# Fixed places in a block for rotation, norm steps and turns; POOL's weight splits in halves; fill 4.2: a hybrid attention and S5 block

## The chip, the cores and the metric

One core of a Trainium2 chip. The metric is the device time of one execution in microseconds (us), the median of several runs. Everything is float32; matrix products run in a three-product scheme (below).

## The reference

One layer over x (1024 tokens × 1024 channels). Beside the attention branch it has an S5 branch with its own gate and up projection, which the change doesn't touch.

```python
h = rmsnorm(x) * (1 + scale) + shift                 # adaLN from c
q, k, v, z_a, u, z_s, g_a, g_s = split(h @ w_in)
q, k = partial_rope(q), partial_rope(k)              # 4 heads, 2 parts each, 64 wide
p = softmax(q k^T * 64**-0.5)                        # per part, per head
o = (p[0] - lam * p[1]) @ v                          # v: 128 wide per head
o = rmsnorm(o, g_subln) * (1 - lam_init)
attn_branch = (o * silu(z_a)) @ w_up_attn
merged = sigmoid(g_a) * attn_branch + sigmoid(g_s) * ssm_branch
out = rmsnorm(x + gate * (merged @ w_out), g_final)
```

## The kernel before

The kernel writes its order of work by hand, engine by engine. Its engines are TensorE (PE: matmuls and transposes), VectorE (V in the code, DVE in the profile), ScalarE (A, ACT), GpSimd (G, POOL) and SyncE (SP, whose queue issues most DMAs). Each engine works through its own instructions in program order.

**Products.** Each float32 operand is split into a high part (a copy by ScalarE, rounded) and a low part (the rest, by a subtract), and a product is three matmuls: high × high, high × low, low × high. The helper `split` (L104) does copy and subtract. Weights come through a plan of 1024-column tiles: `w_load` (L166) issues a tile's DMA, `w_split` (L178) splits it on the engine that `w_state["eng"]` names, and `w_ahead` (L200) does both one unit in advance, after the first triple of the running unit. A unit (`unit`, L209) makes 128 rows of a projection in two halves of 512 tokens; each half has 8 triples of matmuls and yields 0.66 after each.

**Main and fill.** `drive` (L233) runs a main generator, whose yields add to a budget, and spends the budget on a fill generator, whose yields take from it. So the fill's matmuls are woven into the main's order on PE at fixed places.

**The attention stage** (`s3_main`, L1523) has 4 heads of 8 blocks; block g = 8h + i holds 128 queries. Its order for block g:

- `qk(g)` (L1410): the scores of both parts (8 matmuls), their maxima by DVE, their exponentials e by ScalarE;
- `mix(g-1)` (L1436) on DVE: a reciprocal, the weight w (wm), and e[0] + w · e[1] over 1024 columns, "the mix" here;
- in odd blocks `pv` (L1460), 24 matmuls for two blocks' outputs of P·V, copied by ScalarE;
- `spot(0)`, fill, `spot(1)`, fill;
- `transpose_w(g-1)` (L1446): 8 transposes of the mix into two PSUM banks (tag `tp`, two buffers), each evacuated by ScalarE (wth) and DVE (wtl);
- fill, `spot(2)`, fill.

The yields of a block are FA ± FD and FB: 3.1 + 1.0 = 4.1 on average up to block 23 (one more in even blocks, one less in odd ones), and 2.45 + 1.0 from block 24 on. Blocks 32 and 33 finish the last mixes and P·V without scores.

**Fill.** In heads 0 to 2 the fill (`s3_fill`, L1401) makes the next head's q, k and v, then five units of the gate g_a, which go to DRAM through tiles tagged `stg`. For q and k each half has a rotation and a cut (`rope_unit`, L1309). The rotation `turn` is a shuffle by DVE and three POOL operations on 128x512 (sh·sin, q·cos, the sum); `cut` is a copy by ScalarE (rh) and a subtract by POOL, and `finish` then issues four DMAs on SP's queue. They are put off: `ev` appends them to the queue `pend` as turn, skip, skip, cut, and `with_pend` (L1303) pops one at every second yield of the fill. `flush` empties the queue at a head's first block. Head 0's q, k and v come ahead of the blocks, on DVE.

**Places in a block.** `spot(s, g)` (L1531) does, in heads 1 to 3: at (block i = 2, s = 0) V's turn `make_v`; at (2, 1) the previous head's output turn `o_turn` (8 transposes into the same two `tp` banks, copied by ScalarE); at each later spot one step of the norm `o_norm` (L1482); at (5, 0) the load of z; at (6, 0) the turn back `o_back` (L1509: 8 transposes, then two DVE operations) and the store to DRAM.

```python
if (i, s) == (2, 1) and h < 4:
    o_turn(h - 1)
    gens[h] = o_norm(h - 1)
elif h in gens and next(gens[h], gens) is gens:
    gens.pop(h)
```

The norm takes squares (ScalarE, two halves through tag `tb`, which the rotation's sh shares), sums (DVE), an inverse square root in twelve steps on 128x8 (three scalings rqv, nri, nry, then three rounds of nrt, nrt, nry) and one product over 128x1024 by POOL.

**The tail** (`s3_tail`, L1586) does the last head's output turn, norm and turn back on DVE, reloads the first three heads, splits them, and spends what fill is left: yields of 3.0 four times, then all. The up projection with w_up_attn follows, then w_out and the final norm.

Of the kernel before, what the change touches and what calls it, by code (L numbers as in the profile page):

```python
# [18 lines left out]
P = 128  # L19
# [47 lines left out]
def tile_hybrid_block(  # L67
# [12 lines left out]
    def mul(o, a, b, e=None):  # L80
        tt(o, a, b, ALU.mult, e)
# [4 lines left out]
    def sub(o, a, b, e=None):  # L86
        tt(o, a, b, ALU.subtract, e)
# [10 lines left out]
    def act(o, i, f, **kw):  # L98
        A.activation(out=o, in_=i, func=f, **kw)  # L99
# [4 lines left out]
    def split(hi, lo, src, lo_eng=None):  # L104
        act(hi, src, AF.Copy)
        sub(lo, src, f32(hi), lo_eng)
# [71 lines left out]
    def w_split():  # L178
        i = w_state["split"]
        if i >= len(plan):  # L180
            return
        r = w_raw.pop(i)
        h = pp.tile([P, 8 * P], F32R, tag="wh", bufs=2, name="wh")
        l = pp.tile([P, 8 * P], F32R, tag="wl", bufs=2, name="wl")
        split(h, l, r, w_state["eng"])
        k = plan[i][2]
        w_hl[i] = tuple(t[:].rearrange("p (k n) -> p k n", k=k) for t in (h, l))
        w_state["split"] += 1
# [1107 lines left out]
    def flush():  # L1296
        while pend:
            pop()

    def skip():  # L1300
        pass

    def with_pend(g, every):  # L1303
        for n, q in enumerate(g):
            if q is not None and n % every == 0:
                pop()
            yield q

    def rope_unit(c0, scale, h, finish):  # L1309
        t = {}  # L1310

        def ev(hf, sl, ps):
            if hf == 0:
                t["q"] = p3.tile([P, S], F32R, tag="ta", bufs=2, name="rq")
            tq = t["q"]
            lo = tq
            q = f32(tq[:, sl])
            e = V if h == 0 else G
            act(q, ps, AF.Copy, scale=scale)

            def turn():
                sh = p3.tile([P, 512], F32, tag="tb", name="rs")
                V.stream_shuffle(out=sh, in_=q, mask=ROPE_SWAP)
                mul(sh, sh, sinT[:, sl], e)
                mul(q, q, cosT[:, sl], e)
                add(q, q, sh, e)

            def cut():
                if hf == 0:
                    t["h"] = p3.tile([P, S], F32R, tag="tc", name="rh")  # L1330
                hi = t["h"]
                act(hi[:, sl], q, AF.Copy)
                sub(lo[:, sl], q, f32(hi[:, sl]), e)
                if h == 0:
                    finish(hi, lo, sl)

            pend.extend([turn, skip, skip, cut])
            if hf == 1 and h > 0:
                pend.append(lambda: finish(t["h"], lo, slice(0, S)))
        yield from unit(c0, 8, hh, hl, ev)  # L1340

    def prep_q(h):
# [67 lines left out]
    def qk(g):  # L1410
        h, i = divmod(g, 8)
        H = heads[h]
        if i == 0:
            flush()
            H["o"] = po.tile([P, S], F32, tag="o", bufs=2, name="o")
            H["zr"] = po.tile([P, 8, 2], F32, tag="zr", bufs=2, name="zr")
        tok = slice(i * P, i * P + P)
        tb = slice(i % 2 * P, i % 2 * P + P)
        nm = po.tile([P, 2], F32, tag="nm", bufs=2, name="nm")
        zz = po.tile([P, 2], F32, tag="zz", bufs=2, name="zz")  # L1420
        es = []
        for cc in range(2):
            sc = ps3.tile([P, S], F32, tag="sc", bufs=2, name="sc")
            for hf in range(2):
                sl = slice(hf * 512, hf * 512 + 512)
                PE.matmul(out=sc[:, sl], lhsT=H["qq"][:, cc, tok], rhs=H["kk"][:, cc, sl], start=True, stop=False)  # L1426
                PE.matmul(out=sc[:, sl], lhsT=qb_t[g // 2][:, cc, tb], rhs=H["kk"][:, cc, sl], start=False, stop=True)  # L1427
            V.tensor_reduce(out=nm[:, cc:cc + 1], in_=sc, axis=AX.X, op=ALU.max, negate=True)  # L1428
            e = p3.tile([P, S], F32, tag="e", bufs=4, name="e")
            act(e, sc, AF.Exp, bias=nm[:, cc:cc + 1], accum_out=zz[:, cc:cc + 1])  # L1430
            es.append(e)
        e_t[g] = (es, zz)
        if g % 2 == 0:
            turn_q(g // 2 + 1)
# [47 lines left out]
    def o_norm(h, e=G, big=None):  # L1482
        H = heads[h]
        on, zr, o = H["on"], H["zr"], H["o"]
        ss = po.tile([P, 8], F32, tag="oss", name="oss")
        z2 = po.tile([P, 8], F32, tag="wm", bufs=2, name="z2")
        for hf in range(2):
            sl = slice(hf * 512, hf * 512 + 512)
            if big is None:
                jk = p3.tile([P, 512], F32, tag="tb", name="sq")  # L1490
            else:
                jk = big[:, sl]
            act(jk, o[:, sl], AF.Square)
            yield
            V.tensor_reduce(out=ss[:, 4 * hf:4 * hf + 4], in_=jk.rearrange("p (t e) -> p t e", t=4) if big is not None
                            else jk[:].rearrange("p (t e) -> p t e", t=4), axis=AX.X, op=ALU.add)
        mul(z2, zr[:, :, 0], zr[:, :, 0])
        mul(ss, ss, z2)
        yield
        res = []  # L1500
        for n, _ in enumerate(rsqrt_gen(po, ss, 8, 1.0 / P, "o", res)):
            if n % 3 == 2:
                yield
        rs = res[0]
        mul(rs, rs, zr[:, :, 0])
        mul(on, on, bc(rs[:], 2, [P, 8, P]), e)
        yield

    def o_back(h):  # L1509
        H = heads.pop(h)  # L1510
        on, of = H["on"], H["of"]
        pss = []
        for hf in range(2):
            ps = ps3.tile([P, 512], F32, tag="tp", bufs=2, name="tp")
            for k in range(4):
                PE.transpose(ps[:, k * P:k * P + P], on[:, hf * 4 + k, :], ident)
            pss.append(ps)
        for hf, ps in enumerate(pss):
            sl = slice(hf * 512, hf * 512 + 512)
            stt(of[:, sl], ps, cols[:, CSUB:CSUB + 1], of[:, sl], ALU.mult, ALU.mult)  # L1520
        return of

    def s3_main():  # L1523
        run_all(with_pend(chain(prep_q(0), prep_k(0), prep_v(0)), 1))
        flush()
        make_v(0)
        w_state["eng"] = G
        NG = 32
        gens = {}

        def spot(s, g):  # L1531
            h, i = divmod(g, 8)
            if g < 8:
                return
            if (i, s) == (2, 0) and h < 4:
                make_v(h)
            if (i, s) == (2, 1) and h < 4:
                o_turn(h - 1)
                gens[h] = o_norm(h - 1)
            elif h in gens and next(gens[h], gens) is gens:  # L1540
                gens.pop(h)
            if (i, s) == (5, 0):
                load_za(h - 1)
            if (i, s) == (6, 0):
                assert h not in gens
                SP.dma_start(out=ofd[h - 1], in_=o_back(h - 1))

        for g in range(NG + 2):
            fa, fb = (FA, FB) if g < 24 else (LA, LB)
            odd = g % 2  # L1550
            fa += FD * (1 - 2 * odd)
            if g < NG:
                qk(g)
            if 1 <= g <= NG:
                mix(g - 1)
            if g >= 3 and odd:
                pv((g - 3) // 2)
            spot(0, g)
            yield fa / 2
            spot(1, g)  # L1560
            yield fa / 2
            if 1 <= g <= NG:
                transpose_w(g - 1)
            yield fb / 2
            spot(2, g)
            yield fb / 2

    FA, FB, FD = 3.1, 1.0, 1.0
    LA, LB = 2.45, 1.0
    fill3 = with_pend(s3_fill(), 2)  # L1570
    drive(s3_main(), fill3)
    p3.release()
    p2.release()
# [12 lines left out]
    def s3_tail():  # L1586
        o_turn(3)
        load_za(3)
        norm = o_norm(3, V, op.tile([P, S], F32, tag="pt", bufs=3, name="sq2"))
        next(norm)  # L1590
        ofl = []
        for h in range(3):
            ofl.append(op.tile([P, S], F32, tag="sg", bufs=3, name="ofl"))
            SP.dma_start(out=ofl[h], in_=ofd[h])
        next(norm)
        yield 3.0
        run_all(norm)
        for h in range(3):
            split(oh[:, h], ol[:, h], ofl[h])
            yield 3.0  # L1600
        of = o_back(3)
        split(oh[:, 3], ol[:, 3], of)
        yield 1000.0
# [124 lines left out]
    def finish(t, rs):  # L1728
        stt(xr[t], xr[t], rs, gf, ALU.mult, ALU.mult)
        SP.dma_start(out=ov[t], in_=xr[t])  # L1730
# [62 lines left out]
```

## Time and profile before

| | us |
|---|---|
| runs | 912.81, 911.06, 912.46 |
| median | 912.46 |
| profiled execution, whole | 911.19 |
| its span, first to last instruction | 909.3 |
| its mean granted clock of PE | 0.989 |
| attention stage, blocks and tail | about 460 to 772 |

The times are those of whole executions. The profile is of one of them, and its microseconds count from the first instruction. Busy times of PE include the overlap of a matmul with the next; a timeline row gives start, length, engine, line, operation, output <- inputs, form and count, and in brackets the idle time of the engine before it and what ended it.

### The profile page before, as it was taken

How to read it: one execution, taken by the hardware profiler on the slowest of the kernel's cores; microseconds unless marked ns; L12 is line 12 of the kernel's file. 1: busy time of each engine (PE TensorE's matmuls, PEld its weight loads, DVE VectorE, ACT ScalarE, POOL GpSimd, SP SyncE). 2: the span in 40 equal slices, each digit the busy share in tenths (PEclk: the TensorE clock that was granted, in tenths of full speed). 3: DMA queues.
4: the chain of work that ended last, by engine and by line, in shares of the span. 5: the costliest groups of instructions: out<-in, count | busy, mean ns of one | idle time of the engine just before them, and what ended most of it. 6: DMA issues, size and time to landing. Idle time of an engine off the chain costs nothing.

```text
span 909.3 us, 12201 instructions
## 1 busy us (share of the span) xinstructions
PE 873.0 (96%) x4528; PEld 732.6 (81%) x4528; DVE 673.3 (74%) x1264; ACT 366.1 (40%) x610; POOL 134.5 (15%) x115
## 2 busy tenths in 40 slices
PE   5999999999999899999999999898999999999996
PEld 4878888888888788787878887787788888887886
DVE  5986999899999976674657767875866756573465
ACT  6754442132222236301246556455555544232222
POOL 1001000000000001000025434423511111350000
PEclk9899899999999999999999999999999999999999
DMA  9936133333243446595433313132232224848022
GB/s 296 307 83 186 52 112 110 101 98 118 85 126 107 125 139 196 207 327 185 123 98 81 91 38 81 64 95 63 70 105 58 81 94 140 333 176 312 12 88 98
DMA packets 107117, 119.56 MB, mean 131 GB/s; under 512 B 7716, under 2 KB 87825, under 8 KB 107059
## 3 DMA queue, kind: packets, MB, share of 16 engines
q1 hardware_dynamic: 105268, 114.08, 40.5%
q10 hardware_dynamic: 1614, 4.51, 1.2%
q8 instruction: 36, 0.59, 0.3%
q0 software_dynamic: 176, 0.20, 0.1%
q14 instruction: 23, 0.18, 0.1%
HBM read 78.46 MB, written 27.73 MB: 117 GB/s over the span
## 4 chain that ended last, share of the span: by engine, by line
PE 41%; DVE 7%; ACT 3%; DMA 2%; issue 2%; POOL 2%; SPq 0%; ACTq 0%; DVEq 0%; POOLq 0%
PE mm L217 19%; PE op L1712 9%; PE pv L1468 4%; PE tp L1457 3%; PE sc L1427 3%; PE sc L1426 2%; DVE nm L1428 2%; POOL pta L78 1%; DVE e L96 1%; ACT e L99 1%; DVE wtl L78 1%; DMA wor<-in_w_out_dram 1%; DMA pad<-pt 1%; ACT mh L99 1%; DMA pta<-pad 1%
## 5 line engine op out<-in xcount | busy, mean ns | idle before, releaser
L217 PE MATMUL mm<-hh,wh 128*128 128x512 f32 x592 | 239.1, 404 | 0.0
L217 PE MATMUL mm<-hh,wl 128*128 128x512 f32 x592 | 232.6, 393 | 2.9 <-DVE wl L78 2.8
L217 PE MATMUL mm<-hl,wh 128*128 128x512 f32 x592 | 232.6, 393 | 0.0
L217 PEld LDWEIGHTS mm<-hh,wl 128*128 128x128 f32 x592 | 112.1, 189 | 28.2 <-DVE wl L78 4.1
L217 PEld LDWEIGHTS mm<-hh,wh 128*128 128x128 f32 x592 | 112.3, 190 | 22.4 <-issue 1.7
L217 PEld LDWEIGHTS mm<-hl,wh 128*128 128x128 f32 x592 | 112.5, 190 | 20.4
L99 ACT ACTIVATE e<-sc,nm 128x1024 f32<-128x1024 f32 x64 | 71.2, 1115 | 77.1 <-DVE nm L1428 77.0
L1428 DVE TENSOR_REDUCE nm<-sc 128x1 f32<-128x1024 f32 x64 | 75.3, 1218 | 14.2 <-PE sc L1427 13.1
L78 DVE TENSOR_TENSOR wtl<-tp,wth 128x512 fp32r<-128x512 f32 x64 | 41.2, 686 | 60.0 <-ACT wth L99 59.9
L99 ACT ACTIVATE wh<-wr 128x1024 fp32r<-128x1024 f32 x49 | 51.7, 1056 | 62.0 <-DMA wr<-in_w_in_dram 24.2
L99 ACT ACTIVATE side<-mm 128x512 f32<-128x512 f32 x48 | 28.7, 598 | 112.8 <-PE mm L217 78.5
L78 POOL TENSOR_TENSOR wl<-wr,wh 128x1024 fp32r<-128x1024 f32 x14 | 34.7, 2477 | 207.2 <-ACT wh L99 207.0
L78 DVE TENSOR_TENSOR wl<-wr,wh 128x1024 fp32r<-128x1024 f32 x35 | 42.9, 1227 | 29.2 <-ACT wh L99 29.0
L1712 PE MATMUL op<-woh,ml 128*128 128x512 f32 (+1 forms) x136 | 51.3, 377 | 1.1 <-DVE ml L78 1.1
L1712 PE MATMUL op<-wol,mh 128*128 128x512 f32 (+1 forms) x136 | 51.2, 377 | 0.0
L1712 PE MATMUL op<-woh,mh 128*128 128x512 f32 (+1 forms) x136 | 51.2, 377 | 0.0
L99 ACT ACTIVATE wth<-tp 128x512 fp32r<-128x512 f32 x64 | 34.8, 596 | 40.1 <-PE tp L1457 40.1
L1426 PE MATMUL sc<-kk,qq 128*128 128x512 f32 x128 | 49.9, 390 | 0.0
L1427 PE MATMUL sc<-kk,qb 128*128 128x512 f32 x128 | 49.9, 390 | 0.0
L96 DVE SCALAR_TENSOR_TENSOR e<-e,wm 128x1024 f32<-128x1024 f32 x32 | 45.3, 1415 | 1.1
L1468 PE MATMUL pv<-wth,vh 128*128 128x256 f32 x128 | 36.5, 285 | 2.7 <-DVE wtl L78 2.7
L1457 PE MATMUL tp<-cst,e 128*128 128x128 f32 x256 | 33.3, 273 | 5.8 <-DVE nry L78 2.4
(365 smaller groups left out, 1693.1 us busy)
## 6 DMA issues: line engine op xcount, KB each, us to landing
wr<-in_w_in_dram SPq DMA_DIRECT2D x40, 512.0 KB
wa<-in_w_ada_dram SPq DMA_DIRECT2D x16, 512.0 KB
x<-in_x_dram SPq DMA_DIRECT2D x8, 512.0 KB
gsd<-side SPq DMA_DIRECT2D x8, 512.0 KB
gad<-side SPq DMA_DIRECT2D x8, 512.0 KB
gt<-gsd SPq DMA_DIRECT2D x8, 512.0 KB
wg<-in_w_ada_dram SPq DMA_DIRECT2D x8, 512.0 KB
pad<-pt ACTq DMA_DIRECT2D x8, 512.0 KB
```

The costliest lines, as they stand in the source:

```text
L78: (e or V).tensor_tensor(out=o, in0=a, in1=b, op=op)
L96: V.scalar_tensor_tensor(out=o, in0=a, scalar=s, in1=b, op0=op0, op1=op1)
L99: A.activation(out=o, in_=i, func=f, **kw)
L217: PE.matmul(out=ps, lhsT=a[:, k, off:off + P], rhs=r[:, k, sl], start=(n == 0), stop=(n == 3 * K - 1))
L1426: PE.matmul(out=sc[:, sl], lhsT=H["qq"][:, cc, tok], rhs=H["kk"][:, cc, sl], start=True, stop=False)
L1427: PE.matmul(out=sc[:, sl], lhsT=qb_t[g // 2][:, cc, tb], rhs=H["kk"][:, cc, sl], start=False, stop=True)
L1428: V.tensor_reduce(out=nm[:, cc:cc + 1], in_=sc, axis=AX.X, op=ALU.max, negate=True)
L1457: PE.transpose(ps[:, k, :], e[:, kt * P:kt * P + P], ident)
L1468: PE.matmul(out=ps[:, 0:256], lhsT=a[:, kt, :], rhs=r[:, kt, :], start=(n == 0), stop=(n == 23))
L1712: PE.matmul(out=ps[:, 0:n], lhsT=a[:, k, tok], rhs=r[:, k, lo:lo + n], start=(i == 0), stop=(i == 23))
```

## The change

- `w_split`: where the split is POOL's, its subtract is made in two operations of 512 columns instead of one of 1024.
- `rope_unit`, heads 1 to 3: each half appends one turn and one cut (with `finish` in the second half's cut). The fill is no longer wrapped in `with_pend`. `pop_turn` at s = 0 of every block runs what is queued up to and including the next turn; `pop_cut` at s = 2 of blocks i = 5 to 7 runs a cut if it is first.
- `spot`: the norm's nine steps stand at nine given places (`STEPS`) of blocks 3 to 7; the output turn goes to (3, 1), the load of z to (7, 0), the turn back with its store to (0, 0) of the next head. `o_norm` has one more yield, and the tail one more `next`.
- FA is 3.2, so a block's yields are 4.2 on average up to block 23.

```diff
@@ w_split
-        split(h, l, r, w_state["eng"])
+        act(h, r, AF.Copy)
+        if w_state["eng"] is G:
+            for j in range(0, 8 * P, 512):
+                sub(l[:, j:j + 512], r[:, j:j + 512], f32(h[:, j:j + 512]), G)
+        else:
+            sub(l, r, f32(h))
@@ behind skip
+    def pop_turn():
+        while pend:
+            kind, fn = pend.popleft()
+            fn()
+            if kind == "turn":
+                break
+
+    def pop_cut():
+        if pend and pend[0][0] == "cut":
+            pend.popleft()[1]()
@@ rope_unit, ev
-            pend.extend([turn, skip, skip, cut])
-            if hf == 1 and h > 0:
-                pend.append(lambda: finish(t["h"], lo, slice(0, S)))
+            def cut_all():
+                cut()
+                if hf == 1:
+                    finish(t["h"], lo, slice(0, S))
+
+            pend.extend([turn, skip, skip, cut] if h == 0 else [("turn", turn), ("cut", cut_all)])
@@ qk
-            flush()
+            while pend:
+                pop_turn()
@@ o_norm
-        z2 = po.tile([P, 8], F32, tag="wm", bufs=2, name="z2")
...
             act(jk, o[:, sl], AF.Square)
             yield
+            if hf == 1:
+                z2 = po.tile([P, 8], F32, tag="wm", bufs=2, name="z2")
             V.tensor_reduce(out=ss[:, 4 * hf:4 * hf + 4], in_=jk.rearrange("p (t e) -> p t e", t=4) if big is not None
                             else jk[:].rearrange("p (t e) -> p t e", t=4), axis=AX.X, op=ALU.add)
+            if hf == 0:
+                yield
@@ s3_main
+        STEPS = ((3, 2), (4, 0), (4, 2), (5, 0), (5, 1), (6, 0), (6, 1), (7, 0), (7, 1))
+
         def spot(s, g):
             h, i = divmod(g, 8)
-            if g < 8:
+            if 1 <= h < 4 and (i, s) in STEPS:
+                next(gens[h], None)
+            if s == 0:
+                pop_turn()
+            if s == 2 and i >= 5:
+                pop_cut()
+            if (i, s) == (0, 0) and h >= 2:
+                SP.dma_start(out=ofd[h - 2], in_=o_back(h - 2))
+            if not 1 <= h < 4:
                 return
-            if (i, s) == (2, 0) and h < 4:
+            if (i, s) == (2, 0):
                 make_v(h)
-            if (i, s) == (2, 1) and h < 4:
+            if (i, s) == (3, 1):
                 o_turn(h - 1)
                 gens[h] = o_norm(h - 1)
-            elif h in gens and next(gens[h], gens) is gens:
-                gens.pop(h)
-            if (i, s) == (5, 0):
+            if (i, s) == (7, 0):
                 load_za(h - 1)
-            if (i, s) == (6, 0):
-                assert h not in gens
-                SP.dma_start(out=ofd[h - 1], in_=o_back(h - 1))
@@ behind s3_main
-    FA, FB, FD = 3.1, 1.0, 1.0
+    FA, FB, FD = 3.2, 1.0, 1.0
     LA, LB = 2.45, 1.0
-    fill3 = with_pend(s3_fill(), 2)
+    fill3 = s3_fill()
@@ s3_tail
         next(norm)
+        next(norm)
         yield 3.0
```

## Rows read from the trace of the kernel before

**Rows 1.** The page, part 1: busy time, share of the span, instructions
```profile
PE 873.0 (96%) x4528; PEld 732.6 (81%) x4528; DVE 673.3 (74%) x1264; ACT 366.1 (40%) x610; POOL 134.5 (15%) x115
```

**Rows 2.** Stretches by windows: length, busy of each engine, clock, DMA share, GB/s
```profile
460.00:752.00 292.00, 280.26 (x1570) 239.71 (x1569) 206.46 (x313) 156.37 (x278) 98.37 (x64) 1.00 0.28 76
```

**Rows 3.** Waits of PE, 455 to 752 us: total us, times, longest us
```profile
PE tp L1479 <- DVE vl L78: 3.2, 3, 1.1
PE pv L1468 <- DVE wtl L78: 2.7, 3, 2.0
PE tp L1457 <- DVE nry L78: 2.4, 2, 1.7
PE tp L1457 <- DVE nrt L78: 2.2, 2, 1.3
```

**Rows 4.** Timeline of PE in block 1: start us, us, engine, line, operation
```profile
467.01 0.39 PE L1426 MATMUL sc<-kk,qq 128*128 128x512 f32 x1
...
470.63 0.39 PE L217 MATMUL mm<-hh,wl 128*128 128x512 f32 x1
472.17 1.09 PE L1457 MATMUL tp<-cst,e 128*128 128x128 f32 x8 [1.15 <-DVE e L96]
```

**Rows 5.** Timeline of POOL in block 12
```profile
566.30 1.29 POOL L78 TENSOR_TENSOR rq<-rq,rs 128x512 f32<-128x512 f32 x1
568.58 2.43 POOL L78 TENSOR_TENSOR wl<-wr,wh 128x1024 fp32r<-128x1024 f32 x1 [0.99 <-ACT wh L99]
```

**Rows 6.** Timeline of DVE in block 12
```profile
566.27 2.40 DVE L96 SCALAR_TENSOR_TENSOR e<-e,wm 128x1024 f32<-128x1024 f32 x1
...
568.78 2.25 DVE L96 SCALAR_TENSOR_TENSOR nrt<-nrt,rqv 128x8 f32<-128x8 f32 x1
```

**Rows 7.** Timeline of DVE in block 1
```profile
468.11 2.35 DVE L1428 TENSOR_REDUCE nm<-sc 128x1 f32<-128x1024 f32 x2 [4.60 <-PE sc L1427]
...
470.83 1.28 DVE L96 SCALAR_TENSOR_TENSOR e<-e,wm 128x1024 f32<-128x1024 f32 x1
```

**Rows 8.** Timeline of DVE at 639 to 645 us, POOL in a rotation from 639.40
```profile
639.23 1.26 DVE L78 TENSOR_TENSOR wtl<-tp,wth 128x512 fp32r<-128x512 f32 x2
...
640.76 1.22 DVE L91 TENSOR_SCALAR nri<-rqv 128x8 int32<-128x8 int32 x1
...
642.09 2.35 DVE L1428 TENSOR_REDUCE nm<-sc 128x1 f32<-128x1024 f32 x2
```

**Rows 9.** The chain that ended last, in order of time: start us, us, what
```profile
589.69 0.87 PE tp L1457 x8
...
593.08 2.87 PE pv L1468 x24
```

**Rows 10.** Groups of POOL by line and form: busy us, mean ns of one, idle before
```profile
L78 POOL TENSOR_TENSOR wl<-wr,wh 128x1024 fp32r<-128x1024 f32 x14 | 34.7, 2477 | 207.2 <-ACT wh L99 207.0
```

**Rows 11.** Timelines at 649 to 652 us, POOL's row first, then DVE's two
```profile
650.80 1.31 POOL L78 TENSOR_TENSOR rs<-rs,sinT 128x512 f32<-128x512 f32 x1
...
649.66 1.22 DVE L96 SCALAR_TENSOR_TENSOR nrt<-nrt,rqv 128x8 f32<-128x8 f32 x1
650.91 1.22 DVE L96 SCALAR_TENSOR_TENSOR nry<-nrt,nry 128x8 f32<-128x8 f32 x1
```

**Rows 12.** Groups of ACT by line, 455 to 752 us
```profile
L99 ACT ACTIVATE e<-sc,nm 128x1024 f32<-128x1024 f32 x64 | 71.2, 1115 | 77.1 <-DVE nm L1428 77.0
...
L99 ACT ACTIVATE rh<-rq 128x512 fp32r<-128x512 f32 x12 | 7.5, 629 | 5.4 <-POOL rq L78 5.4
```

**Rows 13.** Timelines at the stage's end: PE (two rows), then DVE (two rows)
```profile
739.64 1.03 PE L1457 MATMUL tp<-cst,e 128*128 128x128 f32 x8
...
767.63 0.48 PE L217 MATMUL mm<-hh,wh 128*128 128x512 f32 x1
...
740.96 1.29 DVE L78 TENSOR_TENSOR wtl<-tp,wth 128x512 fp32r<-128x512 f32 x2 [2.29 <-ACT wth L99]
...
770.02 1.23 DVE L78 TENSOR_TENSOR ol<-of,oh 128x1024 fp32r<-128x1024 f32 x1 [1.13 <-ACT oh L99]
```

## The prediction

> **What bounds the kernel now.** I began with the page's busy times: TensorE (PE) is busy 96% of the span, DVE 74%, and PEld (81%) only overlaps PE [rows 1]. So a change pays where PE stands still. The stretches by windows show that the attention stage has such time: from 460 to 752 us PE is busy 280.26 of 292.00 us, 11.7 us idle, at a granted clock of 1.00 [rows 2]. The waits of PE give the causes [rows 3]: 3.2 us (3 times) for the subtract that frees the banks of V's turn, 2.7 us (3) for the lower part of the weights of P·V, 2.4 and 2.2 us (2 each) put down to small steps of the norm (nry, nrt); one mix adds 1.15 us [rows 4]. A matmul is drawn 0.39 us long but the next starts 0.23 us later, so each stall takes 0.16 us more than its idle time: the transposes at 472.17 could have begun at 470.86 [rows 4]. These 11 stalls are 11.65 + 11 × 0.16 = 13.4 us, the ceiling of what the change can win here.
>
> Why is VectorE (DVE) late? At 566.30 GpSimd (POOL) makes the third operation of a rotation, 1.29 us, and at 568.58 a weight split of 2.43 us [rows 5]. The mix that DVE starts at 566.27 takes 2.40 us, where the one at 470.83 with POOL idle took 1.28: it ends 1.08 us after POOL's operation. The 128x8 step at 568.78 takes 2.25 us and ends with the weight split, at 571.0 [rows 5 to 7]. So a DVE operation with two inputs in SBUF stands until POOL's instruction is over. A scaling (tensor_scalar) does so too, 1.22 us at 640.76; but the reduction of the scores from PSUM (2 × 1.18) and the subtract wtl with one input in PSUM (2 × 0.63) keep their speed beside POOL [rows 8]. PE stalls only where the mix ends after PE has reached the transposes; the stalls of 1.3 and 1.7 us put down to nrt and nry are of this kind, the named step standing just behind a blocked mix.
>
> **A block's timetable.** Counted from its first score matmul (467.01), the first maximum starts at 1.1 us and the mix lasts from 3.8 to 5.1 us [rows 4, 7]. Eight score matmuls take 1.8 us and a triple of fill 0.69 us at 0.23 a matmul; eight transposes 0.87, P·V (odd blocks) 2.87 us [rows 9]. The loop that hands out fill gives, at 4.2 a block, at least 6 triples ahead of the transposes in an even block and mostly 3 or 4 in an odd one, 8 and 5 in the whole block. So transposes are due at 1.8 + 6 × 0.69 = 6.0 us (even) and 1.8 + 2.9 + 3 × 0.69 = 6.8 us (odd), 0.9 and 1.7 us after an unhindered mix; the blocks last 8.2 and 9.0 us.
>
> **What it removes.**
> - The output turn goes from right behind V's turn (block 2) to block 3, behind P·V and two triples of fill. The bank it then needs is freed by ScalarE's copy of P·V, and 1.4 us of fill covers that. Gain 3.2 + 3 × 0.16 = 3.7 us [rows 3].
> - The rotation starts behind the mix. Its shuffle ends at about 5.9 us, POOL's three operations at 9.8 us; the next mix is due at 8.2 + 3.8 = 12.0 us or later, and what lies beside POOL, wtl and the maxima, doesn't wait. The norm's steps stand behind the mix too. The other seven stalls go, the last P·V's because two triples instead of one now stand ahead of it: 2.7 + 2.4 + 2.2 + 7 × 0.16 = 8.4 us [rows 3].
> - Fill 4.2 gives block 1 four triples instead of three ahead of its transposes: 0.7 of the 1.31 us at 472.17 [rows 4].
> Sum removed: 12.8 us. The matmuls stay the same in number, so none of it is paid back as PE work.
>
> **What it adds.**
> - POOL's weight split in two: 2 × 1.29 for 2.48 us, 0.1 us more each of 14 times [rows 5, 10]. POOL is busy 98 of 292 us [rows 2], so nothing on the path. A DVE step behind it waits 1.3 us at most, if it gets in between the halves: at 650.9 one did, between two POOL operations back to back, and the next step waited for the second [rows 11].
> - Block 13 (head 1). In block 12 POOL has a cut (1.3), a rotation (3.9) and a weight split (2.6): the cut's copy on ScalarE (0.63) follows two exponentials of 1.12 [rows 12], so POOL is at work from about 5.5 to 13.2 us, 5.0 us into block 13. The mix there waits 1.1 us and ends at 6.1 (due at 6.8: harmless). Then come a reduction of 0.7 us, two products, one of them behind the next cut's subtract (to 8.0), and the shuffle (to 9.0); then three scalings behind the rotation, as at 640.76: I count two full waits, 2.8 us in all. So wtl ends at 13.1 us, 4.1 into block 14; two maxima (2.35) and the mix bring DVE to 8.1 where transposes are due at 6.0: 2.1 us. The ends are 0 (POOL early) and 3.5 (one POOL operation more); I take the worked value. In head 2 no split falls there, and the same sum ends where seven triples make it due: 0.
> - The tail. The fill that the loop leaves to it falls from 22 triples to 19, just what it spends ahead of the last turn back. Today nine matmuls of fill follow that turn from 767.63, then nine of the up projection's first three heads; the last head's lower part is ready at 770.02 + 1.23 = 771.25 [rows 13]. Without the fill PE asks for it ten matmuls after 767.63, at 770.0: 1.2 us, between 0.9 and 1.5.
> - Block 32 has no scores ahead of the third turn back. PE comes there at about 741.2; wtl frees the two banks at 741.6 and 742.25 [rows 13]: 0.6 us (0 to 1.0). The earlier two stand behind scores: nothing.
> - V's turn has a cut's copy of 0.63 us ahead of it on ScalarE; PE's six triples cover it. Nothing, at worst 1.0 us over three heads.
> - Queues. On SP's the load of z is issued a block ahead of its use, as before; heads are stored at the next head's block 0, the last in block 32, still ahead of its reload in the tail. The eight loads of qq and kk wait there for the cuts, as now, with 10 us to spare; the q loads and weight loads behind them are for later blocks. On ScalarE the squares and the last cut wait for a rotation's end, up to 2.5 us into the next block; behind them stands an exponential, due at 2.4 and mixed a block later. Nothing; without that block of slack some 0.6 us each.
> Sum added: 3.9 us. Net: −8.9 us.
>
> The profiled execution took 911.2 us, 1.3 below the median of the runs (912.5). 911.2 − 8.9 = 902.3; against the median 903.6, my number.
>
> **Rivals.**
> 1. Waits move instead of going. For it: in block 5 of heads 1 and 2 the norm's steps still meet a rotation. If blocks 14 and 22 both stall 3.5 us, 8.8 us come back with the tail and block 32: −4.0, or 908.5; with those and V's turn at their upper ends 10.5 come back: 910.2. Against: head 2 has no split there. The Trainium skill (Perfetto Trace Analysis, Optimization Strategy) reads a gap that repeats as too few buffers; by that the turn's stall, which the trace does show three times, would go along to block 3 and the sum would give 907.3. I keep the 3.7, since the bank there is freed early. Chance 0.2.
> 2. Slower. POOL's chain in a rotation block (cut, rotation, split: up to 7.8 of 8.2 to 9.0 us) slips until it lies on the next mix. Mixes so blocked cost 1.3 + 0.16 and 1.7 + 0.16, 1.66 us in the mean [rows 3]. That decides from 7 blocks on ((12.8 − 1.8) / 1.66); with nine of the twelve rotations hit it is 14.9 + 1.8 − 12.8 = +3.9: 916.4. Against: few of the twelve have a split behind them. Chance 0.08.
> 3. Nothing comes out: the stage gets shorter, but the up projection then waits for its loads. They are issued behind the tail and should move along with it. 912.5; chance 0.07.
>
> **How the numbers follow.** The forecast has 0.65: from all added costs at their lower ends (0.9: 900.6) to all at their upper ends with block 13 once (7.0: 906.7). The range reaches into rival 1, 900 to 909; left out are rivals 2 and 3 and rival 1's far end, some 0.2. About 0.2% (1.8 us) is what a measurement of this kernel can tell from no change. Faster by more than that are forecast and rival 1, 0.85; within it rival 3, 0.07; slower rival 2, 0.08.
>
> **What would show it.** Right: PE idle for about 4 us from 460 us to the tail's start; no wait on vl; mixes of 1.28 us in rotation blocks but for block 13; weight splits in pairs of 1.3 us; a stall at block 14's transposes; a wait of about 1.2 us on ol in the up projection's first unit. Wrong: PE waiting on mixes in several rotation blocks, POOL operations lying on mixes, or a gain in the stage that the up projection's waits take back.

## The result, and the profile after

The changed kernel takes 901.14 us in the median against 912.62 of the kernel before beside it: ratio 0.988, 95% interval 0.986 to 0.989. One of its four executions took 2726.32 us, and no run shows why; the ratio and its interval go by the other three, whose median is 901.04. A second measurement gave 901.6 against 911.92, 0.989 (0.987 to 0.990). The forecast was 903.6, with a range of 900 to 909. The profiled execution's span fell from 909.3 to 899.4 us.

Part 1 of the page and the group of POOL's weight splits; the rows answer to [rows 1] and [rows 10]:

```profile
PE 871.4 (97%) x4528; PEld 732.7 (81%) x4528; DVE 668.8 (74%) x1264; ACT 366.1 (41%) x610; POOL 135.1 (15%) x129
...
L78 POOL TENSOR_TENSOR wl<-wr,wh 128x512 fp32r<-128x512 f32 x28 | 35.6, 1291 | 157.0 <-ACT wh L99 156.9
```

The 4528 matmuls are the same, the 14 splits are 28 halves of 1.29 us. PE's busy time hardly moved: what went is time in which it stood. The same stretch as in [rows 2], by windows, shows it:

```profile
460.00:752.00 292.00, 289.87 (x1626) 250.07 (x1625) 208.06 (x329) 163.16 (x286) 102.38 (x79) 1.00 0.30 85
```

2.1 us idle where 11.7 were. The waits of PE from 455 to 775 us, all there are (total us, times, longest; against [rows 3]):

```profile
PE tp L1477 <- DVE nrt L78: 1.2, 1, 1.2
PE mm L222 <- DVE of L96: 1.2, 1, 1.2
PE tp L1477 <- DVE e L96: 0.5, 1, 0.5
PE tp L1539 <- DVE wtl L78: 0.4, 1, 0.4
PE tp L1412 <- ACT vt L99: 0.2, 1, 0.2
```

No wait is left on vl, none of P·V on wtl. The five rows are, in this order, block 14's transposes, the up projection's first matmul, the rest of block 1's wait, the turn back in block 32, and one wait ahead of the stage that was there before.

Spans differ by some 2 us between executions for reasons outside the stage (last section), so the experiments are read by the length of the stage, from its first score to the first matmul of w_out: 353.65 us before, 343.38 after (343.02 in the second measurement). "Stall" is the idle time plus 0.16 us, as in the prediction.

### The profile page after: what moved, and what is told of

It reads as the page before. It is cut to its first block, busy times and chain, and to the rows that moved or that the text cites. A ratio compares the mean times of both kernels' runs of the same rounds, so it can differ in the third digit from the quotient of the medians.

```text
span 899.4 us, 12216 instructions
## 1 busy us (share of the span) xinstructions
PE 871.4 (97%) x4528; PEld 732.7 (81%) x4528; DVE 668.8 (74%) x1264; ACT 366.1 (41%) x610; POOL 135.1 (15%) x129
## 4 chain that ended last, share of the span: by engine, by line
PE 46%; DVE 4%; issue 4%; ACT 2%; DMA 1%; POOL 1%; ACTq 0%; SPq 0%; DVEq 0%; POOLq 0%
PE mm L222 21%; PE op L1741 9%; PE pv L1488 5%; PE tp L1477 3%; PE sc L1447 3%; PE sc L1446 3%; POOL pta L78 1%; DVE nm L1448 1%; DMA wor<-in_w_out_dram 1%; DMA pad<-pt 1%; ACT mh L99 1%; DVE e L96 1%; PE tp L1499 0%; ACT woh L99 0%; DVE pt L96 0%
## 5 line engine op out<-in xcount | busy, mean ns | idle before, releaser
L78 POOL TENSOR_TENSOR wl<-wr,wh 128x512 fp32r<-128x512 f32 x28 | 35.6, 1291 | 157.0 <-ACT wh L99 156.9
L96 DVE SCALAR_TENSOR_TENSOR e<-e,wm 128x1024 f32<-128x1024 f32 x32 | 42.1, 1314 | 1.1
L1488 PE MATMUL pv<-wth,vl 128*128 128x256 f32 x128 | 36.2, 283 | 0.0
L1488 PE MATMUL pv<-wtl,vh 128*128 128x256 f32 x128 | 36.2, 283 | 0.0
```

The lines of the kernel that those rows point to most:

```text
L78: (e or V).tensor_tensor(out=o, in0=a, in1=b, op=op)
L96: V.scalar_tensor_tensor(out=o, in0=a, scalar=s, in1=b, op0=op0, op1=op1)
L1488: PE.matmul(out=ps[:, 0:256], lhsT=a[:, kt, :], rhs=r[:, kt, :], start=(n == 0), stop=(n == 23))
```

## The experiments

| kernel | turn | rotations | norm's steps | fill | stage us | median us | ratio to before (95%) |
|---|---|---|---|---|---|---|---|
| before | (2, 1) | with the fill | every place | 4.1 | 353.65 | 911.92 to 912.62 | |
| turn alone | (3, 1) | with the fill | every place | 4.1 | 353.81 | 911.43 | 0.9994 (0.998 to 1.001) |
| rotations alone | (2, 1) | fixed | every place | 4.1 | 366.34 | 925.48 | 1.016 (1.013 to 1.019) |
| all but the turn | (2, 1) | fixed | nine places | 4.2 | 350.97 | 907.27 | 0.995 (0.993 to 0.997) |
| all but the rotations | (3, 1) | with the fill | nine places | 4.2 | 346.72 | 903.24 | 0.990 (0.988 to 0.993) |
| all but the norm | (3, 1) | fixed | nine in a row | 4.2 | 348.52 | 906.26 | 0.993 (0.991 to 0.995) |
| all but the fill | (3, 1) | fixed | nine places | 4.1 | 345.95 | 904.63 | 0.991 (0.988 to 0.994) |
| **changed** | (3, 1) | fixed | nine places | 4.2 | 343.38 | 901.14 | 0.988 (0.986 to 0.989) |
| splits whole | (3, 1) | fixed | nine places | 4.2 | 343.30 | 901.1 | 0.987 (0.985 to 0.989) |
| improved | (3, 1) | fixed | nine, moved | 4.2 | 340.24 | 898.87 | 0.985 (0.983 to 0.987) |

### One part taken back

**The output turn**, back right behind V's turn:

```diff
-            if (i, s) == (3, 1):
+            if (i, s) == (2, 1):
                 o_turn(h - 1)
```

> The changed kernel with the output turn alone put back right behind V's turn, at (2, 1). The theory of the prediction: PE waits three times on vl again, 1.1 to 1.6 us each, so 3.7 us more than the changed kernel (901.1), some 904.8. The rival (a gap that comes from too few banks and goes along with the turn): the stall is worth nothing, 901 within 0.7.

The stage took 350.97 us, 7.6 more, and the whole 907.27 us where 904.8 was expected. All three waits on vl are back, and each is longer than before:

```profile
PE tp L1499 <- DVE vl L78: 4.9, 3, 1.7
```

That is 4.9 + 3 × 0.16 = 5.4 us. Behind the third, at 690.71, PE got less than its full clock for some microseconds, shown by windows (the last three columns are the granted clock, the DMA share and GB/s):

```profile
690.50:696.00 5.50, 5.29 (x23) 4.19 (x24) 0.75 (x2) 1.79 (x3) 0.00 (x0) 0.69 0.00 0
```

Eight matmuls there have almost twice the pitch, 1.6 us more. The turn's place is thus worth more than 3.7 us here, 5.4 without the slow clock; the stall does not come along to block 3. A gap that repeats can mean, by the Trainium skill (Perfetto Trace Analysis, Optimization Strategy), that there are too few buffers; here the buffers stayed two and the gap went, because the transposes got work of PE in front of them.

**The rotations**, handed out by the fill again (`fill3 = with_pend(s3_fill(), 2)`, no `pop_turn` and `pop_cut` in `spot`, the rest as changed):

> The changed kernel with rotations and cuts popped by the fill again, one at every second yield, all else as changed. The theory: POOL's rotations lie on mixes again (mixes over 2 us in heads 1 and 2) and PE waits on some of them: 3 to 7 us more, 904 to 908. The rival (the norm's small steps did the damage, and their places alone took it away): at most 1 us more, under 902.2. A second rival (only POOL's halves mattered): no change, 901.

346.72 us, +3.3: by the stage at the theory's lower end (the median, 903.24, lies between theory and rival), but by another way in part. Some mixes are long again (2.3 us, five of them), yet the three longest new stalls, all of transposes and 1.0 to 1.2 us each, come from ScalarE (ACT). Its timeline in head 1, and then PE's row:

```profile
574.17 0.64 ACT L99 ACTIVATE sq<-o 128x512 f32<-128x512 f32 x1 [5.54 <-POOL rq L78]
574.71 1.10 ACT L99 ACTIVATE e<-sc,nm 128x1024 f32<-128x1024 f32 x1
...
576.88 0.38 ACT L99 ACTIVATE o<-pv 128x256 f32<-128x256 f32 x1
```

```profile
577.32 0.66 PE L1476 MATMUL tp<-cst,e 128*128 128x128 f32 x4 [0.82 <-ACT o L99]
```

A square of the norm stands 5.54 us for POOL's rotation, with which its tile shares a buffer; the exponentials and the copy of P·V, which frees the transposes' bank, queue up behind it. Ahead of the other two it was the cut's copy rh that stood so, 5.11 and 5.02 us. The Trainium skill (PSUM — Partial Sum Buffer, Engine vs sequencer instructions) says that ScalarE's queue is strictly first in, first out; the trace agrees, the copy began 2.7 us after the square.

**The norm's steps**, nine places in a row:

```diff
-        STEPS = ((3, 2), (4, 0), (4, 2), (5, 0), (5, 1), (6, 0), (6, 1), (7, 0), (7, 1))
+        STEPS = ((3, 2), (4, 0), (4, 1), (4, 2), (5, 0), (5, 1), (5, 2), (6, 0), (6, 1))
```

> The changed kernel with the norm's nine steps one behind the other at every place from (3, 2) to (6, 1), rotations at their fixed places. The theory: rounds of 128x8 steps now meet rotations in blocks 4 and 5 and the second squares wait on ScalarE in front of wth, so PE stalls in heads 1 and 2: 2 to 6 us more, 903 to 907. The rival (only the rotation's place mattered): 901 within 0.7.

348.52 us, +5.1, and no mix is long. Nearly all of it is one wait of P·V in head 1, 3.8 us, and the six microseconds behind it, at a granted clock of 0.72 in the mean. ScalarE again, with the row of PE's waits behind it:

```profile
571.32 0.63 ACT L99 ACTIVATE sq<-o 128x512 f32<-128x512 f32 x1 [5.35 <-POOL rq L78]
...
573.28 1.07 ACT L99 ACTIVATE wth<-tp 128x512 fp32r<-128x512 f32 x2
```

```profile
PE pv L1488 <- DVE wtl L78: 3.8, 1, 3.8
```

The second square now stands in front of the copy of the weights, wth. PE's wait names wtl, which ran on DVE right behind wth: the engine named is the last link, not the cause.

**The fill**, back at 4.1 (`FA` 3.1):

> The changed kernel with fill 4.1. The theory: the tail has 22 triples again and its 1.3 us wait goes, block 1 has 3 triples and its stall grows by 0.7; with what the other blocks lose at random, 0.6 us less, 900.5 (899.5 to 902). The rival (4.2 is what keeps the mixes ahead of the transposes): stalls in rotation blocks, 1 to 3 us more, 902 to 904.

345.95 us, +2.6: the theory's −0.6 missed, and the rival held by the stage (the median, 904.63, is 0.6 us above its range). The tail's wait went and block 1's is 1.31 again, as worked out; but there are new stalls of 0.8 us in block 16 and 1.7 in block 22. With less fill a block the units of the fill slip against the blocks, and the weight splits fall elsewhere. POOL's timeline and PE's row at the first of them:

```profile
591.21 2.54 POOL L78 TENSOR_TENSOR wl<-wr,wh 128x512 fp32r<-128x512 f32 x2 [10.67 <-ACT wh L99]
593.69 1.91 POOL L78 TENSOR_TENSOR o<-o,nry 128x1024 f32<-128x1024 f32 x1
```

```profile
595.65 1.09 PE L1539 MATMUL tp<-cst,o 128*128 128x128 f32 x8 [0.67 <-POOL o L78]
```

A split stands in front of the norm's product, and the turn back waits for that. In head 2 a split now falls in front of block 21's mix, which takes 2.28 us, as block 13's does in head 1.

**The weight splits**, whole again:

```diff
-            for j in range(0, 8 * P, 512):
-                sub(l[:, j:j + 512], r[:, j:j + 512], f32(h[:, j:j + 512]), G)
+            sub(l, r, f32(h), G)
```

> POOL's weight split in one operation of 1024 columns again, the rest as changed. Theory (the halves are nothing on the path): POOL has 3 us or more of room in nearly every block, so the attention stage keeps its 343.4 us within 1 us, the time its 901.1 within 2 us. The DVE steps that meet a split wait up to 2.5 us instead of 1.3, but only block 13's stand near PE's path, and there the split comes ahead of the cut in either case. Rival (the halves matter): a step of the norm or a mix behind a whole split stands 1.2 us longer and PE's transposes of block 14 or 22 feel it: stall there of 2.5 us or one more stall of 1 to 2 us, +1 to +3 us.

343.30 us against 343.38, and up to w_out the same stalls to 0.01 us: the halves cost and gain nothing on the path, as forecast.

### One part alone

**The turn alone**, in the kernel before:

```diff
-            if (i, s) == (2, 1) and h < 4:
+            if (i, s) == (3, 1) and h < 4:
...
-            if (i, s) == (5, 0):
+            if (i, s) == (6, 0):
                 load_za(h - 1)
-            if (i, s) == (6, 0):
+            if (i, s) == (7, 0):
...
             act(jk, o[:, sl], AF.Square)
-            yield
             V.tensor_reduce(...)
+            yield
```

> The kernel before with one part of the change alone: the output turn at (3, 1) instead of (2, 1), with everything that follows it (norm steps, load of z, turn back) one block later; the square and its sum stand in one step, rotations stay with the fill, 4.1. Theory (the turn's three stalls are its own, whatever else is done): the waits on vl go with the small gaps right behind them, -3.7 to -4.2 us; the norm's steps meet other rotations, so the other seven stalls (9.2 us) change their places and may come to 7 to 11: 906 to 910.5 against 912.5. Rival (the turn only pays together with the fixed rotations): P.V's copy that frees the bank is late behind ScalarE's waits for rotations, the turn waits at its new place, -1 us or less.

The three waits on vl are gone, and the stage is no shorter: 353.81 us. The rival had the amount, but no wait came at the turn's new place. So half of the theory holds; what the other stalls would take was bounded too low: they come to 10.6 us where 7 to 11 were expected, and a slow clock takes some 1.4 us more. P·V's wait at 629.93 grew from 2.0 to 4.3 us, and PE had a granted clock of 0.59 for four microseconds behind it (by windows); waits at late mixes are there as before, in other blocks (1.7, 1.5 and 1.3 us). ScalarE shows why; first the kernel before, then this one:

```profile
630.05 0.63 ACT L99 ACTIVATE rh<-rq 128x512 fp32r<-128x512 f32 x1 [5.38 <-POOL rq L78]
630.58 1.07 ACT L99 ACTIVATE wth<-tp 128x512 fp32r<-128x512 f32 x2
```

```profile
628.04 0.63 ACT L99 ACTIVATE rh<-rq 128x512 fp32r<-128x512 f32 x1 [6.29 <-POOL rq L78]
628.57 1.06 ACT L99 ACTIVATE wth<-tp 128x512 fp32r<-128x512 f32 x2
```

```profile
629.80:633.80 4.00, 3.87 (x21) 3.87 (x22) 3.93 (x7) 2.10 (x3) 0.21 (x1) 0.59 0.98 229
```

The cut's copy rh waits for a rotation, and wth stands behind it. With the turn and its stall no longer in front, PE reaches P·V 4.3 us earlier (625.65 for 629.93); the weights come only 2.0 us earlier, and the wait takes up the rest.

**The rotations alone**, from the changed kernel: turn at (2, 1), norm's steps at nine places in a row from (2, 2), load of z and turn back in blocks 5 and 6, fill 4.1.

> The changed kernel with only the rotations and cuts (and the halves of the weight splits) left as changed: turn at (2, 1), norm steps one at every place from (2, 2) on, load of z at (5, 0), turn back at (6, 0), fill 4.1. Theory (a mix is late only when a rotation lies on it, and the norm's steps at every place still push the weights of P.V and the mixes): mixes of 1.3 us nearly everywhere, the three waits on vl stay (3.7 us), of the other seven stalls (9.2 us) 4 to 6 stay as in the run with free norm steps, so -3 to -5 us: 907.5 to 909.5. Rival (the rotation is the whole cause of the seven stalls): they all go, -8 to -9 us: 904.

925.48 us, 13 slower than before; both theories missed. The mixes are short but for two, as the theory had it, but PE waits; its three longest rows from 455 to 775 us are these:

```profile
PE tp L1539 <- POOL o L78: 6.7, 2, 3.4
PE tp L1477 <- DVE rqv L93: 6.4, 2, 3.4
PE tp L1499 <- DVE vl L78: 4.2, 3, 1.6
```

The second row is the square again, which at 563.44 had stood 5.38 us for a rotation in front of wth. The first is the turn back at its old place, block 6: POOL's product that it needs is queued behind that block's rotation, as POOL's timeline in head 1 shows:

```profile
583.05 1.30 POOL L78 TENSOR_TENSOR rs<-rs,sinT 128x512 f32<-128x512 f32 x1
584.31 1.28 POOL L78 TENSOR_TENSOR rq<-rq,cosT 128x512 f32<-128x512 f32 x1
585.68 1.26 POOL L78 TENSOR_TENSOR rq<-rq,rs 128x512 f32<-128x512 f32 x1
586.89 1.89 POOL L78 TENSOR_TENSOR o<-o,nry 128x1024 f32<-128x1024 f32 x1
```

So a fixed place for the rotation pays only if the norm's squares, its product and the turn back get places that suit it. No run takes back the turn back's new place, or the load of z's, by itself. Taken back singly, turn, rotations, norm and fill cost 7.6 + 3.3 + 5.1 + 2.6 = 18.6 us of the stage, where the whole change brings 10.3: the parts can't be added up.

### What was left, taken out

**Block 14.** One norm step taken out of block 5's rotation, the later ones moved on:

```diff
-        STEPS = ((3, 2), (4, 0), (4, 2), (5, 0), (5, 1), (6, 0), (6, 1), (7, 0), (7, 1))
+        STEPS = ((3, 2), (4, 0), (4, 2), (5, 0), (6, 0), (6, 1), (6, 2), (7, 0), (7, 1))
```

> The norm's fourth to ninth steps moved: nothing at the second place of block 5 of a head, where POOL is in a rotation; instead one step more at the last place of block 6. Theory (block 14's stall comes from the three scalings that stand behind block 13's rotation and so push the weights of P.V and the next mix): the stall of 1.39 us ahead of block 14's transposes goes, no other comes, -1.4 us: 899.7. Rival (it comes from block 13's own late mix of 2.2 us): the stall stays within 0.3 us, time as changed. Other rival: the steps moved to block 6 meet that block's rotation and stall block 15, 0 to -0.5 us net.

The wait on nrt is gone from the list, no other came; stage 341.88 us, −1.5 (899.33 us in all). This settles the cause: the mix of block 13 takes 2.21 us here too and ends 6.0 us into its block, as in the changed kernel, and there is no stall. So it isn't the mix of block 13 but the scalings behind it, as the forecast had it. DVE's timeline in the changed kernel, from that mix (block 13's first score starts at 568.98):

```profile
572.80 2.22 DVE L96 SCALAR_TENSOR_TENSOR e<-e,wm 128x1024 f32<-128x1024 f32 x1
574.94 0.67 DVE L1516 TENSOR_REDUCE oss<-sq 128x4 f32<-128x512 f32 x1
575.54 0.98 DVE L78 TENSOR_TENSOR z<-zr 128x8 f32<-128x8 f32 x1
...
576.64 0.73 DVE L1339 STREAM_SHUFFLE rs<-rq 128x512 f32<-128x512 f32 x1
577.27 0.16 DVE L93 TENSOR_SCALAR rqv<-oss 128x8 f32<-128x8 f32 x1
577.47 1.31 DVE L91 TENSOR_SCALAR nri<-rqv 128x8 int32<-128x8 int32 x1
578.81 1.21 DVE L93 TENSOR_SCALAR nry<-nri 128x8 int32<-128x8 int32 x1
579.94 1.28 DVE L78 TENSOR_TENSOR wtl<-tp,wth 128x512 fp32r<-128x512 f32 x2
581.14 2.34 DVE L1448 TENSOR_REDUCE nm<-sc 128x1 f32<-128x1024 f32 x2
...
583.84 1.28 DVE L96 SCALAR_TENSOR_TENSOR e<-e,wm 128x1024 f32<-128x1024 f32 x1
```

and with the steps moved, where wtl follows the shuffle at once and ends at 577.61 instead of 581.22 (spans shifted by 0.95):

```profile
575.70 0.76 DVE L1339 STREAM_SHUFFLE rs<-rq 128x512 f32<-128x512 f32 x1
576.33 1.28 DVE L78 TENSOR_TENSOR wtl<-tp,wth 128x512 fp32r<-128x512 f32 x2
```

**The stage's end.** The turn back of block 32 behind fill, and smaller portions of fill in the tail, so that some is left behind the last turn back:

```diff
-            if (i, s) == (0, 0) and h >= 2:
+            if (i, s) == (0, 0 if h < 4 else 1) and h >= 2:
...
-        yield 3.0
+        yield 2.4
...
-            yield 3.0
+            yield 2.4
```

> Two edits: the turn back of head 2 in block 32 goes from that block's first place to its second, behind fill; and the tail's four portions of fill are 2.4 instead of 3.0, so about three triples are left behind the last turn back. Theory (the turn back waits for P.V's weights to leave the two banks, 0.6 us; the up projection asks for the last head's lower part 1.3 us early because no fill is left behind the turn back): 0.6 goes, and of the 1.3 about 0.9, as less fill ahead may let the tail's earlier waits show: -1.5 us, 899.6. Rival (the tail is a chain of DVE from the last P.V to the lower part, whatever PE does between): the fill moved behind leaves an equal wait ahead of the last turn back, -0.6 us alone or nothing.

341.63 us, −1.75 (899.84 us in all): the stall of 0.60 is gone and that of 1.32 is 0.24. PE at the end of the tail, changed kernel and this one:

```profile
757.30 1.03 PE L1539 MATMUL tp<-cst,o 128*128 128x128 f32 x8
759.50 0.47 PE L222 MATMUL mm<-oh,wh 128*128 128x512 f32 x1 [1.16 <-DVE of L96]
```

```profile
753.95 1.03 PE L1539 MATMUL tp<-cst,o 128*128 128x128 f32 x8
754.74 0.48 PE L222 MATMUL mm<-hh,wh 128*128 128x512 f32 x1
...
757.80 0.47 PE L222 MATMUL mm<-oh,wh 128*128 128x512 f32 x1
```

What PE waits for here is not the last head's part, though. DVE's and ScalarE's rows in the changed kernel:

```profile
757.94 1.41 DVE L96 SCALAR_TENSOR_TENSOR of<-tp,cols,of 128x512 f32<-128x512 f32 x2 [0.98 <-PE tp L1539]
759.38 1.06 ACT L99 ACTIVATE oh<-of 128x1024 fp32r<-128x1024 f32 x1 [5.73 <-DVE of L96]
```

PE's first matmul with oh starts at 759.50, 0.15 us behind the end of `of` and before that head's high part is made; in this run it starts at 757.80, 0.14 us behind the end of `of` (757.66). `of` reads the last turn back out of the two `tp` banks. In the code the stage's PSUM pool is released there (`ps3.release()`) and the up projection's is opened, so the wait is probably for those banks; no run changes this.

**Both:**

> The moved norm steps and the two edits of the stage's end together. Theory: the two gains lie at different places of PE's order and add, -2.9 us against the changed kernel: 898.2, attention stage from first score to first matmul of w_out about 340.5 us. Rival: the stalls come back at the next place (w_out's first operands, ready 0.4 to 1.3 us late already), so that the stage ends no more than 1.5 us earlier: 899.6.

340.24 us, −3.14, where the two alone bring 1.50 and 1.75: they add, all but 0.1. For the time of a whole execution the two kernels ran once more on one chip:

> The changed kernel as it is, on the same chip as the run with moved norm steps and turn back, to compare the two directly. Both theories: 901.1 us as before, within 1.5 us; attention stage 343.4 us from first score to first matmul of w_out, within 0.5.

> The moved norm steps and the two edits of the stage's end together, once more, beside the changed kernel. Theory (the three stalls they remove are 1.39, 0.60 and 1.32 us, and nothing takes their place): stage 340.2 us, time 2.5 to 3.5 us under the changed kernel's on this chip. Rival (the 2.3 us seen between the medians so far were the chips'): less than 1.5 us between them, though the stage in the trace is shorter.

901.6 and 897.81 us, 3.8 apart, a little over the 2.5 to 3.5 expected; ratios to before 0.989 (0.987 to 0.990) and 0.984 (0.982 to 0.986) do not overlap, and the stages are 343.02 and 340.43, 2.6 apart. So this version is faster than both kernels. Of its stage 460 to 752 us PE is idle for 0.5:

```profile
460.00:752.00 292.00, 291.53 (x1635) 251.87 (x1636) 207.23 (x332) 164.72 (x289) 103.31 (x79) 1.00 0.30 85
```

## Why the prediction was right, and where it wasn't

- **Removed 12.8.** Up to 752 us there were 13.4 us of stalls; of them 0.63 is left, at block 1, where 0.6 was to be left. 12.8, as worked out.
- **Block 14, 2.1 us: mis-sized, 1.39** (1.05 in the second measurement). POOL was done 4.95 us into block 13 (5.0 forecast) and the mix at 6.0 (6.1). The product behind the cut's subtract ended at 7.5, not 8.0; of the three scalings two waited, 2.5 us where 2.8 were counted; so wtl ended 0.9 us earlier than worked out.
- **Tail, 1.2: 1.32, but by another wait.** I had PE wait for the last head's low part, ol, ten matmuls into the up projection. It waits at the first one, for `of` (above), a wait that I had not seen. ol was done at 761.71, and PE came to it at 761.85, just in time because it had stood before. Without that it would have come there at about 760.5 (an estimate from the pitch of 0.23 us) and stood some 1.2 us: the wait that I named is hidden behind another of the same size, and that the amount came out is luck.
- **Block 32, 0.6: 0.60; V's turn, POOL's halves, queues, 0: 0.**
- **Sum.** Stalls: −12.8 + 3.3 = −9.5, for −8.9 forecast. The stage became 0.8 us shorter than that. Pauses of up to 0.11 us right behind a stall (the turn's second bank, P·V's second matmul) went with it; I hadn't counted them. The span fell by 9.9, the median by 11.5; the rest lies in what differs from execution to execution.
- **The step that failed is the cause of the stalls.** I wrote that VectorE is late because POOL holds its operations, for the stalls besides the turn's. For those of 1.28 and 1.70 us behind mixes of 2.40 and 2.39 us it was so, and for the two in head 2 (0.94 and 0.75 us), where the mixes were plain but norm steps of 1.22 us had stood in front of the maxima [rows 8, 11]. For the longest, 2.0 + 0.16 us at P·V, it was ScalarE: rh stood 5.38 us for POOL's rotation [rows 12] with wth behind it, and DVE was idle for 7.43 us. DVE's row and PE's in the kernel before:

```profile
631.20 1.29 DVE L78 TENSOR_TENSOR wtl<-tp,wth 128x512 fp32r<-128x512 f32 x2 [7.43 <-ACT wth L99]
631.94 0.39 PE L1468 MATMUL pv<-wth,vh 128*128 128x256 f32 x1 [2.01 <-DVE wtl L78]
```

  I had looked at ScalarE's waits in the new order only, and put them at nothing. In the new order that is true (they last 0.35 to 3.4 us, and no wait of PE comes from them), but this queue is behind the longest new wait of every run that takes back the rotations (1.0 us) or the norm (3.8), and of both parts alone (4.3 and 3.4).
- **The turn's 3.7 is a gain only in company.** Alone it gave nothing (with the norm's steps a block later), because the next wait on the path was due at a time of its own. My sum had each stall go by itself; it came out because all that were late went together.
- **Rivals.** Waits moving (1): only the part foreseen in block 14. Slower by POOL's chain on the mixes (2): one of twelve rotation blocks had a long mix, and it is not on the path; but the rotations alone are 13 us slower by POOL's order in another way, in front of the norm's product and the squares. Nothing (3): the up projection has no wait but that at its first matmul; from w_out's first matmul to the end it is 96.05 us before and 96.24 after.

## What to carry to other kernels

A wait that names one engine is to be followed back until an engine stood idle for something that is not its own work: here PE's wait on a DVE subtract was a ScalarE copy that stood behind another copy, which waited for POOL. Where steps of several chains are woven into one order by hand, their places are one decision: a part tried alone can give nothing (the turn) or lose (the rotations), and all parts together pay. Last, whoever keeps the bound engine busy by fill should see how much is left where the next stage waits for its first bank or operand.

## What the runs showed of the hardware

- **A long stall costs more than its length.** After PE had stood 3 to 4.3 us, its granted clock was 0.59 to 0.72 for the next 4 to 6 us, so part of that stretch ran at 1.2 instead of 2.4 GHz: matmuls of 512 columns started 0.43 us apart instead of 0.23. In the run with rotations alone, the wait of 3.4 us at 571.29 and the 5 us behind it:

```profile
564.00:571.20 7.20, 3.85 (x18) 2.85 (x16) 6.02 (x11) 4.33 (x10) 0.00 (x0) 1.00 0.00 0
571.20:576.20 5.00, 4.91 (x19) 4.36 (x20) 4.83 (x12) 2.57 (x5) 3.98 (x4) 0.66 0.73 174
```

  After stalls of 1.7 to 2.2 us it mostly stayed at 1.00 and fell once, at 690.71. Ahead of the attention stage all kernels have a wait of 2.4 to 2.9 us at about 309 to 312 us, and the clock fell behind it in eight of the fourteen profiles. In the changed kernel's first profile it was 0.62 in the 4.5 us from 312.1 on, in the second 1.00, and the stage began at 459.77 and 458.37 us. That alone makes executions of one kernel differ by more than a microsecond, and is why the stage's length served here better than the span. What decides it in one execution stays open.
- **POOL's hold fell on the next two-input operation of DVE, however small.** With whole splits the 128x1 product ahead of block 13's mix took 1.25 us instead of 0.22, and the mix then its plain 1.28:

```profile
572.35 1.25 DVE L96 SCALAR_TENSOR_TENSOR wm<-zr,zz,lamc 128x1 f32<-128x1 f32 x1
573.64 1.28 DVE L96 SCALAR_TENSOR_TENSOR e<-e,wm 128x1024 f32<-128x1024 f32 x1
```

  POOL's split ended at 573.59 there and at 573.93 in the changed kernel, the mix at 574.92 and 575.02: here the end of POOL's operation counted, not which of DVE's stood for it.
